# adaLN weights as one transfer per unit in two tiles, and the units placed at half chunks and partly in later sub-layers

## The chip, the cores and the metric

The kernel runs on one core of one Trainium2 chip. The time is the device time of one execution in microseconds (us). It was 2662.07 us before the change, the median of three runs that lie between 2660.03 and 2666.98 us. The profile is of one further execution, which took 2658.19 us. Engines are named as in the profile: PE (TensorE, with PEld for its weight loads), DVE (VectorE), ACT (ScalarE), POOL (GpSimd), SP (SyncE, which here only issues transfers).

## The reference

One inference step of two layers, for 512 prompt tokens and 8 sequences of 8 sample tokens that share all weights, so 576 tokens of width 1024 in float32. Each layer has three sub-layers: a SwiGLU FFN (`d_ff` 2816), a token mixer (layer 0 a Mamba-2 mixer, layer 1 sliding-window attention), and a second FFN. Every sub-layer is wrapped in norms that are modulated by the conditioning vector c of the sequence:

```python
cs = jax.nn.silu(c)
mod = (cs @ ada_w[i] + ada_b[i]).reshape(bsz, 1, N_SUB, 3, D_MODEL)      # shift, scale, gate of 3 sub-layers
hin = rms_norm(x, norm_pre[i, s]) * (1 + mod[:, :, s, 1]) + mod[:, :, s, 0]
f = swiglu(hin, ffn_w_in[i, si], ffn_w_out[i, si])                       # or the mixer, for s == 1
x = x + coef * mod[:, :, s, 2] * rms_norm(f, norm_post[i, s])            # coef 0.5 for an FFN, 1 for a mixer
```

The change concerns only `cs @ ada_w[i]`, the adaLN modulation: for each layer a matrix of 1024 x 9216 float32, 37.7 MB, which has to be read once and multiplied by nine vectors (one prompt, eight samples).

## The kernel before

**Stages.** The six sub-layers run one after another. They are named by layer and place: (0,0) is the first FFN of layer 0, (0,1) the Mamba mixer, (0,2) the second FFN, then (1,0), (1,1) (attention) and (1,2). An FFN goes through its 22 blocks of 128 hidden columns in four groups, `FFG`: 5, 5, 6 and 6 blocks. After each group `run_out` multiplies the group's hidden columns by their part of `w_out` and adds that to `f`. All large matrix products are three matmuls per 128x128 block, of a high and a low part of weights and activations (`whi`, `wlo`, made by ACT at line 441 or 607 and by DVE or POOL at line 444 or 603 from a raw tile that SP has loaded).

In the first group each weight block is used directly (`gemm_part` and `gemms`, lines 461 and 473). In the other three groups, 17 blocks, `seven` computes a block of the up and gate product from seven half-size products; here such a block is called a chunk. Its matmuls are those of line 628 (`prod`), 84 per chunk in seven products of 12, in this order: pa, pb, pc, pd, then pa, pc and pd again. The raw tiles `raw` and `rawu` of a chunk, 512 KB each, have two buffers each.

**The adaLN work.** The modulation of a layer is cut into five column groups q: q 0 to 3 have 2048 columns, q 4 has 1024 (only the gate of the third sub-layer). Each is cut into 8 units, one for each 128 rows of `ada_w` (`ada_unit`, line 150). A unit issues its transfers from ACT's queue (line 162), four of [128, 512] (256 KB; 128 KB for q 4) into tiles `adaw` of which there are `NADA` = 7, and after a `yield` does four matmuls (line 165), one for each quarter of the columns, which go to four different 32-row strips of one PSUM bank, `adaps`. The profile counts two PE records for one such matmul, so 8 for a unit. The eighth unit of a group then copies the bank to SBUF on ACT (`adasb`, line 169, which takes one of the seven `adaw` tiles), turns it with PE transposes (`adatp`, line 172) and adds the bias on DVE (`modraw`, line 178).

Group (0, 0) is made by another function at the start (`ada_first`). The others are spread over the FFNs by `during`: before the change 32 units in (0,0), 16 in (0,2) and 24 in (1,0). `Pend` hands them out. Its method `step` is called at certain places of an FFN (lines 510, 713, 714); at each call it adds `rate` = units / `nsteps` to a counter and starts one unit for each whole number in it. Starting a unit means: issue its transfers, then do the matmuls of the unit started before. An FFN has 38 such calls: 4 in the rest of the first group, and two together after each of the 17 chunks. `nsteps` is 40 for an FFN. `pend.flush` (line 717), after the last chunk, starts what is left. In (0,2) the adaLN units alternate with 16 units that copy the attention's bias table (`rel_unit`).

**The end of an FFN.** After the last chunk and the flush, the pool `ada` (with the `adaw` tiles and the scratch of `seven`) is closed, and `Boundary.open` loads the residual x. `run_out` then does the last `w_out` product, with four of its eight weight blocks in borrowed tiles `wx`, and beside it gathers the statistics of the norms on ACT, DVE and POOL (`stat`, lines 324 to 335), from which the next sub-layer's input `hin` is made (`sums`, `update`). Below, the *middle* of an FFN is the stretch from its first matmul of line 628 to the first matmul of its last `w_out` product, and its *tail* the stretch from there to the last matmul of that product.

**Order.** The kernel is written in a tile framework. A planner, with its own costs of instructions, sets the order in which each engine's instructions stand and which of the buffers of a tag each tile gets; an instruction may be moved ahead of its place in the program when its operands and a buffer are free by the planner's clock. At run time each engine takes its instructions in that order, and one that waits holds up what is behind it on its engine.

Of the kernel before, what the change touches and what calls it, by code (L numbers as in the profile page):

```python
# [20 lines left out]
EPS = 1e-6  # L21
NEG = -1e30
FFG = ((0, 5), (5, 5), (10, 6), (16, 6))
NADA = 7
NFINE = 24
PL = ((25, 48, 60), (25, 52, 64))
WR = 4
# [31 lines left out]
def body(ctx: ExitStack, tc: tile.TileContext, A, O):  # L59
# [90 lines left out]
    def ada_unit(l, q, k):  # L150
        n = 2048 if q < 4 else 1024
        if k == 0:
            if l and q == 0:
                mods[l] = keep.tile([128, 72, 9], F32, tag="modraw", name="modraw", bufs=2)
            mods[l, q] = ps_a.tile([128, 512], F32, tag="a", name="adaps")
        w = n // 4
        pt = mods[l, q]
        aw = []
        for j in range(4):
            c = q * 2048 + j * w  # L160
            aw.append(ap[0].tile([128, 512], F32, tag="adaw", name="adaw", bufs=NADA)[:, :w])
            nc.scalar.dma_start(aw[j], A["ada_w"][l, k * 128:(k + 1) * 128, c:c + w])
        yield
        for j in range(4):
            PE.matmul(out=pt[32 * j:32 * j + 32, :w], lhsT=cs[:, k, :], rhs=aw[j], start=(k == 0), stop=(k == 7))  # L165
        if k == 7:
            nt = w // 128
            sb = ap[0].tile([128, 512], F32, tag="adaw", name="adasb", bufs=NADA)
            S.copy(sb[:, :w], pt[:, :w])
            tp = ps_s.tile([128, 512], F32, tag="s", name="adatp")  # L170
            for t in range(nt):
                PE.transpose(tp[:, t * 128:(t + 1) * 128], sb[:, t * 128:(t + 1) * 128], ident)
            c0 = q * 16
            md = mods[l][:, c0:c0 + 4 * nt, :].rearrange("p (j t) s -> p t j s", t=nt)
            src = tp[:, :w].rearrange("p (t j s) -> p t j s", j=4, s=32)
            bia = adab[:, l, c0:c0 + 4 * nt].rearrange("p (j t) -> p t j", t=nt)
            for t in range(nt):
                V.tensor_tensor(out=md[:, t], in0=src[:, t, :, 0:9], in1=bia[:, t].unsqueeze(2).to_broadcast([128, 4, 9]),
                                op=ALU.add)
# [88 lines left out]

    def rel_table(pool):

        tab = pool.tile([128, 512], F32, tag="adaw", name="tab", bufs=NADA)[0:16, 0:HL]
        V.memset(tab, NEG)
        p = ps_s.tile([128, 512], F32, tag="s", name="tabp")
        PE.matmul(out=p[0:16, 0:129], lhsT=rb, rhs=oh, start=True, stop=True)
        V.tensor_copy(out=tab[:, 127:256], in_=p[0:16, 0:129])
        nc.scalar.dma_start(scr_t, tab)
# [312 lines left out]
        acts = lambda x: [(x[0][:, k], x[1][:, k]) for k in range(4)]  # L589
        return dict(b11=acts(b11), b21=acts(b21), b22=acts(b22), t1=acts(t1), t2=acts(t2), t3=acts(t3), t4=acts(b12))  # L590

    def seven(pool, mp, l, si, m, acts, mt):

        rg = wp.tile([128, 1024], F32, tag="raw", name="raw", bufs=2)
        ru = pool.tile([128, 1024], F32, tag="rawu", name="rawu", bufs=2)
        for i, r in enumerate((rg, ru)):
            nc.sync.dma_start(r, A["w_in"][l, si, m, :, i])
        a11, a12, a21, a22 = rg[:, 0:512], rg[:, 512:1024], ru[:, 0:512], ru[:, 512:1024]
        sc = pool.tile([128, 2048], F32, tag="scmb", name="scmb")
        s2, s1, s3, s4 = (sc[:, i * 512:i * 512 + 512] for i in range(4))  # L600

        def tt(e, out, a, b, op):
            e.tensor_tensor(out=out, in0=a, in1=b, op=op)  # L603

        def parts(w, c, src):
            n = src.shape[-1]
            S.copy(w[0][:, c:c + n], src)  # L607
            tt(V, w[1][:, c:c + n], src, w[0][:, c:c + n].bitcast(F32), ALU.subtract)

        ws = [[wp.tile([128, 1024], F32R, tag=t, name=t, bufs=WR) for t in ("whi", "wlo")] for _ in range(4)]  # L610
        parts(ws[0], 0, a11)
        tt(V, s1, a21, a22, ALU.add)
        tt(V, s3, a11, a21, ALU.subtract)
        tt(V, s2, s1, a11, ALU.subtract)
        parts(ws[0], 512, s2)
        parts(ws[1], 0, sc[:, 512:1536])
        tt(V, s4, a12, s2, ALU.subtract)
        parts(ws[2], 0, a12)
        parts(ws[2], 512, s4)
        parts(ws[3], 0, a22)  # L620
        pa, pb, pc, pd = (ps_g.tile([128, 512], F32, tag="g", name="g")[:, 0:N2] for _ in range(4))

        def prod(p, w, c, at, first):
            hi, lo = ws[w]
            for k in range(4):
                o = slice(c + k * 128, c + k * 128 + 128)
                for j, (wt, x) in enumerate(((lo, at[k][0]), (hi, at[k][1]), (hi, at[k][0]))):
                    mms.append(PE.matmul(out=p, lhsT=wt[:, o], rhs=x, start=(first and k == j == 0),  # L628
                                         stop=(k == 3 and j == 2), skip_group_check=True))

        def tile_(name):
            return pool.tile([128, N2], F32, tag="cmb", name=name, bufs=5)

        p1, u2, ur, ul = map(tile_, ("p1", "u2", "ur", "ul"))
        gl, gr = (mp.tile([128, 320], F32, tag="sil", name=n, bufs=3)[:, 0:N2] for n in ("gl", "gr"))

        def mid(t, g, u):
            hi, lo = (mt[:, j, t * N2:t * N2 + N2] for j in (0, 1))
            tt(V, u, g, u, ALU.mult)
            S.copy(hi, u)  # L640
            tt(V, lo, u, hi.bitcast(F32), ALU.subtract)

        prod(pa, 0, 0, acts["b11"], True)
        S.copy(p1, pa)
        prod(pb, 0, 512, acts["t2"], True)
        tt(V, u2, pb, p1, ALU.add)
        prod(pc, 1, 0, acts["t1"], True)
        tt(V, ur, pc, u2, ALU.add)
        prod(pd, 1, 512, acts["t3"], True)
        tt(V, ur, pd, ur, ALU.add)  # L650
        prod(pa, 2, 0, acts["b21"], False)
        S.activation(out=gl, in_=pa, func=AF.Silu)
        prod(pc, 2, 512, acts["b22"], False)
        tt(V, gr, pc, u2, ALU.add)
        S.activation(out=gr, in_=gr, func=AF.Silu)
        mid(1, gr, ur)
        prod(pd, 3, 0, acts["t4"], False)
        tt(V, ul, pd, u2, ALU.add)
        mid(0, gl, ul)


    def ffn(l, s, hin, f, pend, bd):
        si = 0 if s == 0 else 1
        sub = lambda name: tc.tile_pool(name=f"{name}{l}{s}", bufs=1, reuse_waits="tile")
        with sub("mid") as mp:
            hin_t = hins[-1]
            for gi, (m0, mk) in enumerate(FFG):
# [24 lines left out]
                if gi == 0:  # L692
                    for m in range(m0, m0 + mk):
                        items += mk_items(m)
                    with sub("fx") as fx:
                        run_in(hin, items[:FI], FI, borrow(fx, "wx", 2 * (FI - WR)), pend,
                               (lambda: first_half1(fx)) if (l, s) == (0, 0) else None,
                               pre if (l, s) == (0, 0) else ())
                    spill((l, s) != (0, 0))
                    ada_cm = sub("ada")  # L700
                    ap[0] = ada_cm.__enter__()
                    if (l, s) == (0, 0):
                        for t, a in later:
                            nc.sync.dma_start(t, a)
                    if (l, s) == (0, 2):
                        rel_table(ap[0])
                    run_in(hin, items[FI:], 0, None, pend)
                    acts = seven_acts(ap[0], hin_t)
                else:
                    for m in range(m0, m0 + mk):  # L710
                        mids.append(mp.tile([128, 2, T], F32R, tag="mid", name="mid", bufs=6))
                        seven(ap[0], mp, l, si, m, acts, mids[-1])
                        pend.step()
                        pend.step()
                if gi < len(FFG) - 1:
                    run_out(loads, halves(mids), f, gi == 0)
# [721 lines left out]

    def x_sums(h):
        t0, n = HALF[h]  # L1440
        xacc = tmp.tile([128, 320], F32, tag="dg", name="xacc", bufs=2)
        for k in range(8):
            sq_add(xacc[:, 0:256], x[h][:, k, :], 256, k == 0)
            if h == 1:
                sq_add(xacc[:, 256:n], x[2][:, k, :], 64, k == 0)
        nb = len(offsets(n))
        ps = ps_s.tile([128, 512], F32, tag="s", name="ssq")
        token_sums(ps, 0, xacc[:, :n], n)
        V.tensor_scalar(out=sx[h], in0=ps[:, :nb], scalar1=1.0 / 1024, scalar2=None, op0=ALU.mult)
        v = small("v0")[:, :nb]  # L1450
        G.tensor_tensor(out=v, in0=sx[h], in1=epsc[:, :nb], op=ALU.add)
        return rsqrt(v, nb)
# [17 lines left out]
    def first_half1(pool):  # L1470
# [1 line left out]
        norm_sample(pool, mv, r_half1, hin)  # L1472


    during = {(0, 0): [(0, 1), (0, 2), (0, 3), (0, 4)], (0, 1): [], (0, 2): [(1, 0), (1, 1)],
              (1, 0): [(1, 2), (1, 3), (1, 4)], (1, 1): [], (1, 2): []}
    nsteps = {0: 40, 1: 20, 2: 40}
    for l in range(2):
        for s in range(3):
            us = [u for lq in during[l, s] for u in units(*lq)]  # L1480
# [162 lines left out]
```

## Time and profile before

| | |
|---|---|
| median of three runs | 2662.07 us |
| the profiled execution | 2658.19 us, of which the span from the first to the last instruction is 2656.4 us |
| PE busy | 2500.6 us (94%), mean granted clock 0.966 |
| DVE, ACT, POOL busy | 1820.5 us (69%), 1149.3 us (43%), 344.5 us (13%) |
| HBM read, written | 301.70 MB, 29.67 MB; 125 GB/s over the span |
| transfers into `adaw` | 224 of 256 KB, 64 of 128 KB, all on ACT's queue |

Busy times are sums over the span. A row of the timeline or of the chain of waits begins with its start in us from the span's start and its length; a row of grouped instructions begins with line, engine and operation. "x8" is a count of instructions. A row of busy time by window has the stretch and its length, then the busy us and the instructions of PE, PEld, DVE, ACT and POOL, PE's granted clock as a share of 2.4 GHz, the mean busy share of the 16 DMA engines and GB/s. What stands in square brackets behind a row is the time that the engine was idle before it, and what ended that.

### The profile page before, as it was taken

How to read it: one execution, taken by the hardware profiler on the slowest of the kernel's cores; microseconds unless marked ns; L12 is line 12 of the kernel's file. 1: busy time of each engine (PE TensorE's matmuls, PEld its weight loads, DVE VectorE, ACT ScalarE, POOL GpSimd, SP SyncE). 2: the span in 40 equal slices, each digit the busy share in tenths (PEclk: the TensorE clock that was granted, in tenths of full speed). 3: DMA queues.
4: the chain of work that ended last, by engine and by line, in shares of the span. 5: the costliest groups of instructions: out<-in, count | busy, mean ns of one | idle time of the engine just before them, and what ended most of it. 6: DMA issues, size and time to landing. Idle time of an engine off the chain costs nothing.

```text
span 2656.4 us, 45760 instructions
## 1 busy us (share of the span) xinstructions
PE 2500.6 (94%) x18037; PEld 2301.2 (87%) x18037; DVE 1820.5 (69%) x3361; ACT 1149.3 (43%) x2400; POOL 344.5 (13%) x476
## 2 busy tenths in 40 slices
PE   7999999789999999799999989999988998999997
PEld 5989788677888887799999889899978868999997
DVE  5566656598758677866677585766747677677685
ACT  3343324445545453534343443433443565343343
POOL 2000000432313122600000230000013006000001
PEclk8999999999999999899999989999998998999998
DMA  6444544333443434163343423535334312222323
GB/s 240 147 141 151 173 131 137 110 116 96 138 128 95 137 112 156 62 194 125 123 159 112 137 103 118 171 131 166 104 120 156 109 41 95 96 87 89 96 76 107
DMA packets 150606, 331.13 MB, mean 125 GB/s; under 512 B 21231, under 2 KB 51551, under 8 KB 146943
## 3 DMA queue, kind: packets, MB, share of 16 engines
q1 hardware_dynamic: 100535, 245.52, 28.9%
q10 hardware_dynamic: 49856, 82.69, 9.5%
q8 instruction: 141, 2.31, 0.4%
q14 instruction: 74, 0.61, 0.1%
HBM read 301.70 MB, written 29.67 MB: 125 GB/s over the span
## 4 chain that ended last, share of the span: by engine, by line
PE 77%; DVE 7%; DMA 7%; issue 3%; ACT 3%; POOL 2%; SPq 0%; ACTq 0%; DVEq 0%; POOLq 0%
PE g L473 41%; PE g L628 27%; DMA adaw<-in_ada_w 3%; PE adaps L165 2%; DMA w<-scr_a 1%; DVE st L335 1%; DMA adaf<-in_ada_w 1%; DVE acc L818 1%; POOL wlo L444 1%; POOL stt L331 1%; DVE hin L411 1%; PE po L1255 1%; PE py L902 1%; PE rb L255 1%; DMA raw<-in_w_out 1%
## 5 line engine op out<-in xcount | busy, mean ns | idle before, releaser
L473 PE MATMUL g<-hin,whi 128*128 128x320 f32 (+1 forms) x2880 | 608.9, 307 | 14.3 <-DVE hin L411 14.3
L473 PEld LDWEIGHTS g<-hin,whi 128*128 128x128 f32 x2880 | 481.6, 197 | 24.7 <-DVE hin L411 17.7
L473 PE MATMUL g<-mid,whi 128*128 128x320 f32 (+1 forms) x2432 | 491.8, 297 | 0.0
L473 PE MATMUL g<-hin,wlo 128*128 128x320 f32 (+1 forms) x1440 | 442.3, 312 | 27.5 <-ACT hin L410 10.6
L628 PE MATMUL g<-hin,whi 128*128 128x288 f32 x2176 | 436.3, 294 | 0.0
L473 PEld LDWEIGHTS g<-mid,whi 128*128 128x128 f32 x2432 | 391.8, 189 | 7.7 <-issue 7.0
L473 PE MATMUL g<-mid,wlo 128*128 128x256 f32 (+1 forms) x1216 | 361.0, 298 | 0.1
L628 PEld LDWEIGHTS g<-hin,whi 128*128 128x128 f32 x2176 | 348.9, 188 | 0.0
L628 PE MATMUL g<-tcmb,whi 128*128 128x288 f32 x1632 | 331.6, 297 | 0.0
L628 PE MATMUL g<-hin,wlo 128*128 128x288 f32 x1088 | 325.0, 299 | 0.0
L473 PEld LDWEIGHTS g<-hin,wlo 128*128 128x128 f32 x1440 | 281.0, 197 | 48.4 <-issue 15.5
L441 ACT CAST whi<-raw 128x1024 fp32r<-128x1024 f32 (+2 forms) x220 | 199.2, 906 | 252.4 <-PE g L473 144.5
L444 DVE TENSOR_TENSOR wlo<-raw,whi 128x1024 fp32r<-128x1024 f32 (+3 forms) x200 | 206.2, 1033 | 117.8 <-ACT whi L441 117.0
L628 PEld LDWEIGHTS g<-tcmb,whi 128*128 128x128 f32 x1632 | 265.9, 191 | 8.9 <-issue 8.9
L628 PE MATMUL g<-tcmb,wlo 128*128 128x288 f32 x816 | 243.3, 298 | 0.0
L473 PEld LDWEIGHTS g<-mid,wlo 128*128 128x128 f32 x1216 | 228.7, 188 | 11.3 <-issue 8.7
L628 PEld LDWEIGHTS g<-hin,wlo 128*128 128x128 f32 x1088 | 204.1, 188 | 30.1 <-issue 24.3
L525 DVE TENSOR_TENSOR f<-g,f 128x256 f32<-128x256 f32 (+1 forms) x240 | 108.8, 455 | 159.9 <-PE g L473 158.9
L607 ACT CAST whi<-scmb 128x512 fp32r<-128x512 f32 (+1 forms) x204 | 153.9, 761 | 142.6 <-PE g L628 83.8
L603 DVE TENSOR_TENSOR wlo<-scmb,whi 128x512 fp32r<-128x512 f32 (+1 forms) x204 | 175.1, 865 | 39.7 <-ACT whi L607 39.6
L331 POOL TENSOR_TENSOR st<-x,f 128x256 f32<-128x256 f32 x10 | 10.0, 998 | 1362.1 <-ACT f L325 809.3
L607 ACT CAST whi<-raw 128x512 fp32r<-128x512 f32 x136 | 84.5, 622 | 203.7 <-PE g L628 125.7
(294 smaller groups left out, 4025.4 us busy)
## 6 DMA issues: line engine op xcount, KB each, us to landing
adaw<-in_ada_w ACTq DMA_DIRECT2D x224, 256.0 KB, 5.7
raw<-in_w_in SPq DMA_DIRECT2D x108, 512.0 KB, 3.6
rawu<-in_w_in SPq DMA_DIRECT2D x68, 512.0 KB, 5.3
raw<-in_w_out SPq DMA_DIRECT2D x64, 384.0 KB, 3.1
raw<-in_w_out SPq DMA_DIRECT2D x64, 320.0 KB, 2.9
raw<-in_w_ssm SPq DMA_DIRECT2D x40, 512.0 KB, 3.7
x_dram<-x SPq DMA_DIRECT2D x10, 1024.0 KB, 3.9
x<-x_dram SPq DMA_DIRECT2D x10, 1024.0 KB, 6.7
```

The costliest lines, as they stand in the source:

```text
L165: PE.matmul(out=pt[32 * j:32 * j + 32, :w], lhsT=cs[:, k, :], rhs=aw[j], start=(k == 0), stop=(k == 7))
L255: ins = PE.matmul(out=r[:, c:e], lhsT=mul(y[:, i:i + 1], [128, 128]), rhs=ident[:, 128 - (e - c):128], start=True, stop=True)
L331: G.tensor_tensor(out=st[:, 2, :256], in0=x_cur[h][:, o, :], in1=fs[:, 0:256], op=ALU.mult)
L335: V.tensor_tensor(out=self.acc[h][:, :ns], in0=self.acc[h][:, :ns], in1=st[:, :ns, :n], op=ALU.add)
L411: V.scalar_tensor_tensor(out=hin[h][:, 1, k, :256], in0=tm, scalar=mv["sh"][:, k, 0:1], in1=hin[h][:, 0, k, :256].bitcast(F32), op0=ALU.ad ...
L441: S.copy(hi[:, :n], raw[:, :n])
L444: i = (V if early and c < PSP else eng or V).tensor_tensor(out=lo[:, c:e], in0=raw[:, c:e], in1=hi[:, c:e].bitcast(F32), op=ALU.subtract)
L473: mms.append(PE.matmul(out=p[:, :n], lhsT=wt[:, a:b], rhs=at, start=(k == j == 0), stop=(j == 2 and k == K - 1)))
L525: V.tensor_tensor(out=fs, in0=p, in1=fs, op=ALU.add)
L603: e.tensor_tensor(out=out, in0=a, in1=b, op=op)
L607: S.copy(w[0][:, c:c + n], src)
L628: mms.append(PE.matmul(out=p, lhsT=wt[:, o], rhs=x, start=(first and k == j == 0), stop=(k == 3 and j == 2), skip_group_check=True))
```

## The change

A unit fetches its 128 rows in one transfer of [128, 2048] (1024 KB; 512 KB for q 4) into one of two tiles; the four matmuls read quarters of it. `adasb` gets a tag with one buffer of its own, which `rel_table` uses too. One of the two calls of `step` per chunk moves from the chunk's end to behind its third product (pc), after 36 of the 84 matmuls. `during` now has 24 units in (0,0), 16 in (0,2), 24 in (1,0) and 8 in (1,2): q 4 of either layer is moved to the third sub-layer, the only one that uses it, and one group of layer 1 from (0,2) to (1,0). `nsteps` of an FFN is 34 in place of 40. The tile `xacc` of the start moves from the pool `tmp` to the first `ada` pool.

```diff
-NADA = 7
@@ ada_unit
-        aw = []
-        for j in range(4):
-            c = q * 2048 + j * w
-            aw.append(ap[0].tile([128, 512], F32, tag="adaw", name="adaw", bufs=NADA)[:, :w])
-            nc.scalar.dma_start(aw[j], A["ada_w"][l, k * 128:(k + 1) * 128, c:c + w])
+        aw = ap[0].tile([128, 2048], F32, tag="adaw", name="adaw", bufs=2)[:, :n]
+        nc.scalar.dma_start(aw, A["ada_w"][l, k * 128:(k + 1) * 128, q * 2048:q * 2048 + n])
         yield
         for j in range(4):
-            PE.matmul(out=pt[32 * j:32 * j + 32, :w], lhsT=cs[:, k, :], rhs=aw[j], start=(k == 0), stop=(k == 7))
+            PE.matmul(out=pt[32 * j:32 * j + 32, :w], lhsT=cs[:, k, :], rhs=aw[:, j * w:j * w + w], start=(k == 0),
+                      stop=(k == 7))
...
-            sb = ap[0].tile([128, 512], F32, tag="adaw", name="adasb", bufs=NADA)
+            sb = ap[0].tile([128, 512], F32, tag="adasb", name="adasb", bufs=1)
@@ rel_table
-        tab = pool.tile([128, 512], F32, tag="adaw", name="tab", bufs=NADA)[0:16, 0:HL]
+        tab = pool.tile([128, 512], F32, tag="adasb", name="tab", bufs=1)[0:16, 0:HL]
@@ seven
         prod(pc, 1, 0, acts["t1"], True)
         tt(V, ur, pc, u2, ALU.add)
+        pend.step()
         prod(pd, 1, 512, acts["t3"], True)
@@ ffn
-                        seven(ap[0], mp, l, si, m, acts, mids[-1])
-                        pend.step()
+                        seven(ap[0], mp, l, si, m, acts, mids[-1], pend)
                         pend.step()
@@ x_sums
-        xacc = tmp.tile([128, 320], F32, tag="dg", name="xacc", bufs=2)
+        xacc = ap[0].tile([128, 320], F32, tag="xacc", name="xacc", bufs=2)
@@ body
-    during = {(0, 0): [(0, 1), (0, 2), (0, 3), (0, 4)], (0, 1): [], (0, 2): [(1, 0), (1, 1)],
-              (1, 0): [(1, 2), (1, 3), (1, 4)], (1, 1): [], (1, 2): []}
-    nsteps = {0: 40, 1: 20, 2: 40}
+    during = {(0, 0): [(0, 1), (0, 2), (0, 3)], (0, 1): [], (0, 2): [(0, 4), (1, 0)],
+              (1, 0): [(1, 1), (1, 2), (1, 3)], (1, 1): [], (1, 2): [(1, 4)]}
+    nsteps = {0: 34, 1: 20, 2: 34}
```

## Rows read from the trace of the kernel before

**Rows 1.** The page's chain of work that ended last, by line.

```profile
PE g L473 41%; PE g L628 27%; DMA adaw<-in_ada_w 3%; PE adaps L165 2%; DMA w<-scr_a 1%; DVE st L335 1%; DMA adaf<-in_ada_w 1%; DVE acc L818 1%; POOL wlo L444 1%; POOL stt L331 1%; DVE hin L411 1%; PE po L1255 1%; PE py L902 1%; PE rb L255 1%; DMA raw<-in_w_out 1%
```

**Rows 2.** Busy time by window: middle, tail of (0,0), (0,2), (1,0), (1,2); stretch, length.

```profile
140.27:459.00 318.73, 304.11 (x2185) 271.71 (x2183) 201.06 (x376) 114.26 (x204) 0.00 (x0) 0.98 0.45 147
459.00:522.78 63.78, 52.73 (x341) 44.98 (x339) 27.88 (x46) 25.35 (x55) 23.32 (x30) 0.95 0.39 130
1212.74:1490.25 277.51, 277.51 (x2081) 262.68 (x2079) 199.23 (x366) 113.24 (x203) 0.00 (x0) 1.00 0.41 133
1490.25:1536.90 46.65, 44.28 (x317) 42.78 (x314) 26.35 (x44) 24.45 (x51) 21.35 (x28) 0.96 0.38 134
1657.85:1947.89 290.04, 286.44 (x2140) 265.28 (x2138) 199.15 (x370) 113.72 (x203) 0.00 (x0) 1.00 0.43 140
1947.89:2007.65 59.76, 49.72 (x325) 44.79 (x323) 28.42 (x47) 25.38 (x55) 23.12 (x30) 0.91 0.36 121
2338.22:2598.41 260.19, 260.15 (x1958) 259.47 (x1957) 195.86 (x358) 112.70 (x200) 0.00 (x0) 1.00 0.29 89
2598.41:2642.70 44.29, 41.40 (x298) 40.65 (x296) 24.63 (x52) 18.98 (x38) 3.29 (x3) 0.96 0.32 114
```

**Rows 3.** The same windows, PE's `adaps` matmuls alone: length, busy (records), clock, DMA.

```profile
140.27:459.00 318.73, 35.67 (x214) 0.98 0.45 147
459.00:522.78 63.78, 7.50 (x29) 0.95 0.39 130
1212.74:1490.25 277.51, 15.70 (x118) 1.00 0.41 133
1490.25:1536.90 46.65, 1.11 (x5) 0.96 0.38 134
1657.85:1947.89 290.04, 23.27 (x174) 1.00 0.43 140
```

**Rows 4.** Who waited for the tile `adaw`, whole span: us in total, times.

```profile
  PEld adaps L165: 30.6, 24
  PE adaps L165: 24.1, 23
```

**Rows 5.** PE's timeline at a chunk end of (0,0) with two units.

```profile
163.80 1.92 PE L165 MATMUL adaps<-adaw,cs 128*32 128x512 f32 x14
...
170.41 1.91 PE L165 MATMUL adaps<-adaw,cs 128*32 128x512 f32 x2 [2.64 <-DMA adaw<-in_ada_w]
```

**Rows 6.** ACT's timeline at the same place.

```profile
174.63 0.62 ACT L607 CAST whi<-raw 128x512 fp32r<-128x512 f32 x1 [6.13 <-DMA adaw<-in_ada_w]
```

**Rows 7.** PE's timeline: two neighbouring chunk ends of (0,2), and a half-width unit.

```profile
1223.95 1.06 PE L165 MATMUL adaps<-adaw,cs 128*32 128x512 f32 x8
...
1236.27 1.06 PE L165 MATMUL adaps<-adaw,cs 128*32 128x512 f32 x8
...
1897.83 0.64 PE L165 MATMUL adaps<-adaw,cs 128*32 128x256 f32 x8
```

**Rows 8.** ACT's timeline in the tails of (0,0) and (0,2).

```profile
477.56 0.37 ACT L169 COPY adasb<-adaps 128x256 f32<-128x256 f32 x1 [16.05 <-PE adaps L165]
...
1495.07 0.84 ACT L441 CAST wx<-raw 128x768 fp32r<-128x768 f32 x1 [0.80 <-PE adatp L172]
```

**Rows 9.** The page's transfers of 1 MB: size, median us to landing.

```profile
x_dram<-x SPq DMA_DIRECT2D x10, 1024.0 KB, 3.9
x<-x_dram SPq DMA_DIRECT2D x10, 1024.0 KB, 6.7
```

**Rows 10.** Landing of `rawu`: in chunks of (0,2), then in chunks of (1,2).

```profile
DMA to landing us min/median/max: 3.8/5.4/6.7
...
DMA to landing us min/median/max: 3.6/3.7/4.7
```

**Rows 11.** A `raw` load's issue in SP's timeline, and its first cast in ACT's.

```profile
1223.89 0.33 SPq L597 DMA_DIRECT2D raw<-in_w_in  x1
...
1240.79 0.62 ACT L607 CAST whi<-raw 128x512 fp32r<-128x512 f32 x1 [1.16 <-PE g L628]
```

More of the change, by code (lines that the diff above doesn't have):

```diff
@@ L590, in seven_acts, with seven @@
         return dict(b11=acts(b11), b21=acts(b21), b22=acts(b22), t1=acts(t1), t2=acts(t2), t3=acts(t3), t4=acts(b12))
-    def seven(pool, mp, l, si, m, acts, mt):
+    def seven(pool, mp, l, si, m, acts, mt, pend):
         rg = wp.tile([128, 1024], F32, tag="raw", name="raw", bufs=2)
```

## The prediction

> **What bounds the kernel now.** I read the chain of waits first [rows 1]: 68% of the span is PE in the matmuls of lines 473 and 628, and the adaLN work has two entries, 3% for the landing of `adaw` and 2% for its matmuls. The chain charges a transfer from its issue on, also while PE still works, so 3% (80 us) is too much. The waits on the tile show why to be careful [rows 4]: 24.1 us in 23 stops of PE; the 30.6 us of its weight loads are the same stops seen a second time. But a stop costs more than its idle time, and ACT is held too. So the price of the adaLN work is best read by stage.
>
> For that the busy times by window [rows 2] give a clean ruler: (1,2) has the same FFN without one unit, and its middle takes 260.19 us with PE busy in 260.15. The other middles take 58.5 us more in (0,0), 17.3 in (0,2) and 29.8 in (1,0). Divide by the units in them, eight records each [rows 3]: 214/8 = 26.75 units, 14.75 and 21.75. That is 2.19, 1.17 and 1.37 us for a unit. In (0,2), with one unit per chunk, PE is busy in all of the 277.51 us, so 1.17 us is a unit without any stall (1.06 us of matmuls [rows 7], a bubble, and its share of the transposes). In (0,0) a unit costs nearly twice that.
>
> PE's timeline there shows how [rows 5]: two units fall together at a chunk's end. Seven matmuls (x14) run at once, the eighth waits 2.64 us, and then takes 1.91 us alone, when four together take 1.06 [rows 7]. Two units need eight tiles and there are seven: the eighth transfer can be issued only when the first tile is free, just before it is needed. ACT issues the transfers in order and is held with them: its next cast comes after 6.13 us idle [rows 6]. The granted clock of that middle is 0.98 against 1.00 [rows 2].
>
> The second place is the tail. It takes 63.78 us in (0,0) and 59.76 in (1,0), against 46.65 in (0,2) [rows 2]. Of the 38 calls of `step`, rates of 0.8 and 0.6 leave two units to the flush and one to be finished. In (0,0) ACT stands 16.05 us idle in front of the copy `adasb` [rows 8], and behind that copy on ACT are the casts of the `wx` weights and the statistics. The copy starts 18.6 us into the tail (477.56 − 459.00); in (0,2) the first `wx` cast, which follows such a copy, starts 4.8 us into it (1495.07 − 1490.25).
>
> **The change part by part.**
>
> *One transfer, two whole tiles.* A tile is now free as soon as its unit's matmuls are over, so the transfer for the unit after next is issued then. That the planner moves an issue up to where its buffer comes free is in the trace: seven tiles were ready at 163.80 [rows 5]. So a unit's transfer has at least two half chunks, one chunk of 12.3 us (1236.27 − 1223.95) [rows 7]. No row has a load of 1 MB in rows of 8 KB into this tile. Nearest are 1 MB transfers of x: 3.9 us written, 6.7 read behind others [rows 9]. Up to 12 us the cost is nothing and no end makes it negative; I take the read, 6.7, and cost 0. What hides it is the 84 matmuls of a chunk; without them it would be 6.7 us per unit. The stalls of (0,0) and (1,0) then go, and what is late next is nothing on PE: DVE, the next busiest engine, has 201 of 319 us. Three issues of four go from ACT's queue as well; ACT is busy 114 of 319 us and off the path, so 0.
>
> *Half chunks.* A unit behind pc costs PE the same four matmuls. After it pd comes, whose bank is its own; DVE's add of pc runs beside it. Extra cost between 0 and 0.11 us per unit (the difference of 1.17 and 1.06, if all of it came twice); (0,2) has its stops between products too, so I take 0. A wait there would hold the casts for the next chunk behind the issue on ACT, but the raw tiles give the casts 16.9 us from issue to use [rows 11].
>
> *Rates and places.* 24, 32, 24 and 8 units over 34 steps are all started by the 34th or 35th of 38 calls and finished one later. None is left to the flush. In the first group's four calls (0,0) now finishes one unit, not two: −1.1 us; (0,2) a half one: −0.4. A unit of q 4 costs 1.17 − (1.06 − 0.64) = 0.75 us [rows 7]. The middles over 260.2 become:
> (0,0): 23 × 1.17 = 27.0 in place of 58.5, −31.5;
> (0,2): 7 × 0.75 + 8 × 1.17 = 14.6 in place of 17.3, −2.7;
> (1,0): 27.0 in place of 29.8, −2.8;
> (1,2): 8 × 0.75, +6.0.
>
> *Tails.* Without units the first cast of `wx` and the statistics no longer stand behind an adaLN copy. (0,2) still has 1.11 us of unit matmuls in its tail [rows 3], so 45.5 us is what such a tail takes clean; (1,2), whose end differs, has 44.29 [rows 2]. That gives −18.3 in (0,0), −14.3 in (1,0), −1.1 in (0,2). Ends: nothing (another wait holds the tail) and −37 (all as (1,2)). I take the first sum, −33.7, since (0,2) runs the same code.
>
> *`adasb`, `tab`, `xacc`.* One buffer more or another pool; each copy waits for the transposes of a group eight units back. 0 from both sides: nothing else uses those buffers at that time.
>
> The sum is −31.5 − 1.1 − 2.7 − 0.4 − 2.8 + 6.0 − 33.7 = −66.2 us. The profiled execution (2658.19, of which 2656.4 span) becomes 2592. It lies 3.9 us below the median of the runs, so against that median I say 2596.
>
> A rule of the Trainium skill speaks against one large transfer: its page "DMA: Bandwidth & Descriptors", section "Queues, rings and completion order", says that an engine takes turns between queue rows packet by packet. By it rows of 8 KB from ACT's queue could take two bytes for each of SP's 4 KB rows while both are in flight, and `rawu` would land, as an estimate, after 3 × 3.7 = 11 us. The trace has today's share: 5.4 us beside 1 MB of `adaw` per chunk, 3.7 without [rows 10]. Both are below the 16.9 us of lead [rows 11], so the sum stands by either.
>
> **The rivals.**
>
> 1. *The lead is half of what I count* (the issue stays at its place in the program, one step ahead). For it: a buffer of 1 MB may be placed by the planner differently from small ones. Against it stands the place of the issues [rows 5]. Then the lead is 36 or 48 of 84 matmuls of 11.15 us, plus the unit: 5.8 or 7.4 us, against 6.7. Of 23 gaps in an FFN 13 are one step long, about six of them the short kind: 0.9 us each in two FFNs, 11 us: 2607. Each further us of landing adds 26: 2630 at the most.
>
> 2. *The tails keep half.* Another wait, the load of x or of `wx`, is nearly as late as the copy was. For it: PE idles in (1,2)'s tail too, 44.29 against 41.40 busy. Against: (0,2). Half of 32.6 is 16: 2612.
>
> 3. *Slower: the weight loads starve.* The 1 MB block in flight delays `raw` and `rawu` of the same chunk past their use. It decides from 16.9 us of landing on. At 19 us each of the 51 chunks with units would wait 2 us: +102 − 66 gives 2698. For it: landing grew from 3.7 to 5.4 with units. Against: the DMA engines are busy 0.41 to 0.45 of the middles [rows 2], and in (0,2) that growth cost PE nothing.
>
> 4. *It does not do what it says*: the planner moves the unit at the half chunk back beside the other. Then two whole tiles are ready at once and nothing stalls: 2600; or the waits return elsewhere: about 2662.
>
> **How the numbers follow.** The forecast has 0.75, rival 1 0.07, rival 2 0.10, rival 3 0.05, rival 4 0.03 (a third of it no change). The forecast's own range is 2584 (all tails as in (1,2), and the runs' own 3 us) to 2606. Rivals 1 and 2 put the upper end at 2626; below 2584 and above 2626 about 0.15 is left. About 0.3% is what a measurement can tell from no change. Faster has 0.92, the same 0.03 (rival 4, or a weak form of rival 3), slower 0.05.
>
> **What would show it.** Right: all `adaps` matmuls in clusters of eight records without idle time before them; middles of about 287, 275, 287 and 266 us; no `adasb` copy in a tail, the first `wx` cast some 5 us into each, and tails near 45.5. Waits on `adaw` under 3 us in all. Rival 1 shows in waits of about 1 us before clusters at half chunks; rival 2 in tails above 52 with another releaser; rival 3 in idle time of ACT's casts behind `raw`. I would be wrong first of all in the tails, where I take one stage's value for two others.

## The result and the profile after

The changed kernel takes 2596.84 us, the median of four runs from 2593.56 to 2598.61, against 2661.45 before (four runs now, 2660.03 to 2666.98): a ratio of 0.9765, interval 0.9748 to 0.9783. The forecast was 2596 us. Its profiled execution took 2598.61 us, of which 2596.8 are span. From one profiled execution to the other that is 59.6 us less, where the sum said 66.2. That the median is met so closely is partly luck, the scatter of single executions: before's profiled one lay 3.3 us below its median, after's lies 1.8 above.

First the page after: the chain by line, then the two kinds of transfers at issue with KB and median us to landing. The entry for the landing of `adaw`, 3% in [rows 1], is gone; a unit's 1 MB lands in 6.7 us, and `rawu` in 4.5.

```profile
PE g L470 41%; PE g L625 29%; PE adaps L161 2%; DVE st L332 1%; DMA adaf<-in_ada_w 1%; DMA w<-scr_a 1%; DVE acc L815 1%; POOL wlo L441 1%; POOL stt L328 1%; DVE wlo L441 1%; DVE hin L408 1%; PE po L1252 1%; PE py L899 1%; ACT whi L438 1%; PE rb L252 1%
...
adaw<-in_ada_w ACTq DMA_DIRECT2D x56, 1024.0 KB, 6.7
...
rawu<-in_w_in SPq DMA_DIRECT2D x68, 512.0 KB, 4.5
```

The same eight windows as [rows 2], in the same order (middle and tail of (0,0), (0,2), (1,0), (1,2)). In the middles PE's busy time is now all of the stretch but for 0.66 us in (0,0), and the clock is 1.00 in each. In the tails of (0,0), (0,2) and (1,0) PE is idle for 4.8 to 5.7 us of 49 and has a clock of 0.93 to 0.97.

```profile
140.16:429.05 288.89, 288.23 (x2155) 265.29 (x2154) 199.45 (x374) 113.16 (x203) 0.00 (x0) 1.00 0.46 156
429.05:478.20 49.15, 44.37 (x312) 43.61 (x311) 29.02 (x46) 26.17 (x54) 21.63 (x30) 0.93 0.37 134
1163.35:1438.76 275.41, 275.40 (x2085) 263.00 (x2083) 198.12 (x366) 112.86 (x202) 0.00 (x0) 1.00 0.37 124
1438.76:1487.76 49.00, 43.31 (x312) 42.29 (x311) 28.93 (x46) 26.13 (x54) 21.66 (x30) 0.97 0.38 134
1605.34:1893.26 287.92, 287.92 (x2155) 265.28 (x2153) 199.46 (x374) 112.98 (x203) 0.00 (x0) 1.00 0.46 157
1893.26:1941.71 48.45, 43.35 (x312) 42.35 (x311) 28.89 (x46) 26.05 (x54) 21.58 (x30) 0.96 0.39 136
2273.11:2539.05 265.94, 265.93 (x2024) 261.27 (x2023) 196.69 (x361) 113.09 (x201) 0.00 (x0) 1.00 0.30 98
2539.05:2583.26 44.21, 41.53 (x298) 40.85 (x296) 24.50 (x52) 18.88 (x38) 3.29 (x3) 0.96 0.30 114
```

The `adaps` matmuls alone in the four middles (stretch, length, busy us and records, clock, DMA share, GB/s), which answer to [rows 3]: 23, 15, 23 and 8 units, and none in a tail.

```profile
140.16:429.05 288.89, 24.30 (x184) 1.00 0.46 156
1163.35:1438.76 275.41, 12.99 (x120) 1.00 0.37 124
1605.34:1893.26 287.92, 24.30 (x184) 1.00 0.46 157
2273.11:2539.05 265.94, 4.91 (x64) 1.00 0.30 98
```

Who waited for `adaw` after, over the span (us, times), and its landing: PE's 24.1 us [rows 4] are gone, and of the 30.6 of its weight loads 0.8 are left. ACT's wait is that of the copy `adasb` for the last matmuls of its group.

```profile
  ACT adasb L166: 10.6, 7
  PEld adaps L161: 0.8, 2
...
DMA to landing us min/median/max: 3.2/6.3/9.4
```

PE's timeline after, at the place of [rows 5]: two units of one chunk, 6 us apart, each in one cluster of 1.06 us without idle time before it. At 404.40 two units still fall together, and even there nothing waits, since both have a tile.

```profile
164.89 1.07 PE L161 MATMUL adaps<-adaw,cs 128*32 128x512 f32 x8
...
170.84 1.06 PE L161 MATMUL adaps<-adaw,cs 128*32 128x512 f32 x8
...
404.40 1.92 PE L161 MATMUL adaps<-adaw,cs 128*32 128x512 f32 x16
```

Where the 59.6 us went, window by window (span to span):

| | predicted | measured |
|---|---|---|
| middles (0,0), (0,2), (1,0), (1,2) | −31.5, −2.7, −2.8, +6.0 | −29.8, −2.1, −2.1, +5.75 |
| tails (0,0), (0,2), (1,0), (1,2) | −18.3, −1.1, −14.3, 0 | −14.6, +2.35, −11.3, −0.1 |
| everything else | −1.5 | −7.6 |

So the middles gave 28.3 us of the 31.0 foreseen, the tails 23.7 of 33.7. "Everything else" is mainly −4.8 from the end of (0,0)'s tail to (0,2)'s middle and −3.4 from the end of (0,2)'s tail to (1,0)'s middle.

### The profile page after: what moved, and what is told of

Same layout as the page of the kernel before. It is cut to its first block, busy times and chain, and to the rows that moved or that the text cites. A ratio compares the mean times of both kernels' runs of the same rounds, so it can differ in the third digit from the quotient of the medians.

```text
span 2596.8 us, 45412 instructions
## 1 busy us (share of the span) xinstructions
PE 2472.2 (95%) x18037; PEld 2292.6 (88%) x18037; DVE 1818.5 (70%) x3361; ACT 1149.6 (44%) x2400; POOL 339.8 (13%) x476
## 4 chain that ended last, share of the span: by engine, by line
PE 79%; DVE 8%; DMA 4%; issue 3%; ACT 3%; POOL 3%; SPq 0%; POOLq 0%; DVEq 0%; ACTq 0%
PE g L470 41%; PE g L625 29%; PE adaps L161 2%; DVE st L332 1%; DMA adaf<-in_ada_w 1%; DMA w<-scr_a 1%; DVE acc L815 1%; POOL wlo L441 1%; POOL stt L328 1%; DVE wlo L441 1%; DVE hin L408 1%; PE po L1252 1%; PE py L899 1%; ACT whi L438 1%; PE rb L252 1%
## 5 line engine op out<-in xcount | busy, mean ns | idle before, releaser
L625 PEld LDWEIGHTS g<-tcmb,wlo 128*128 128x128 f32 x816 | 153.3, 188 | 23.0 <-DVE ur L600 18.4
```

## The experiments

Three questions were open: which part of the change does the work, whether the tails were shortened for the reason given (no unit in the flush), and what holds the tails at 49 us in place of 45.5. All times are medians beside runs of the kernel before on the same chip; the ratio and its interval are against those. "Tails" and "middles" stand in the order (0,0), (0,2), (1,0), (1,2).

### The old places in the new tiles, and the new places in the old tiles

```diff
  (changed kernel)
-    during = {(0, 0): [(0, 1), (0, 2), (0, 3)], (0, 1): [], (0, 2): [(0, 4), (1, 0)],
-              (1, 0): [(1, 1), (1, 2), (1, 3)], (1, 1): [], (1, 2): [(1, 4)]}
-    nsteps = {0: 34, 1: 20, 2: 34}
+    during = {(0, 0): [(0, 1), (0, 2), (0, 3), (0, 4)], (0, 1): [], (0, 2): [(1, 0), (1, 1)],
+              (1, 0): [(1, 2), (1, 3), (1, 4)], (1, 1): [], (1, 2): []}
+    nsteps = {0: 40, 1: 20, 2: 40}
```

> The changed kernel with the units in their old sub-layers and at the old rate (40 steps), all else as changed. My theory: a large part of the gain was the flush that is gone, so the tails of (0,0) and (1,0) grow again, from 49 us to 55 to 64 each, by waits of ACT's adasb copy in the tail; the middles keep their 1.2 us per unit. Time 2612 to 2628. Rival (the tail was long because of the seven tiles, not because of units left over): tails stay within 3 us of 49, time 2595 to 2602.

Measured: 2594.99 us (2594.44 to 2601.22), ratio 0.9737 (0.9696 to 0.9778). My expectation of the time missed; it came out at the lower end of the rival's range. Three windows of this kernel's profile, (0,0)'s tail and (1,2)'s middle and tail, and below them ACT's timeline in (0,0)'s tail:

```profile
435.10:491.98 56.88, 47.29 (x332) 45.63 (x329) 28.50 (x46) 25.15 (x55) 22.12 (x30) 0.91 0.39 135
...
2278.95:2539.16 260.21, 260.20 (x1958) 259.54 (x1957) 195.70 (x358) 112.54 (x200) 0.00 (x0) 1.00 0.28 88
2539.16:2579.07 39.91, 39.85 (x298) 39.30 (x296) 24.25 (x52) 19.01 (x38) 3.30 (x3) 1.00 0.20 67
```

```profile
445.30 0.37 ACT L166 COPY adasb<-adaps 128x256 f32<-128x256 f32 x1 [7.89 <-PE adaps L161]
```

The mechanism that I named is there: the copy `adasb` is back in the tail, 10.2 us into it, and that tail is 7.7 us longer than after's. (1,0)'s, at 50.43, is only 2.0 longer, as the rival said. Against the kernel before, the two tails are 6.9 and 9.3 us shorter with the old places, so a large part of what they gained in the change comes from its other parts. And without units (1,2) is 5.7 us shorter in its middle and 4.3 in its tail, and (0,2)'s tail takes 45.12. The middles and tails add up to 0.9 us less than after's. The new places shift time from these two tails to other windows.

The counterpart, before's kernel with the new `during` and `nsteps` alone:

> The kernel before with only the new sub-layers of the units and 34 steps; seven small tiles and both steps at the chunk's end stay. My theory: the tails lose 24 us as in the changed kernel, (0,0) has 24 full units with about seven pairs in its middle (300 to 305 us), and (1,0) gets the same, 300 to 305 in place of 290; time 2625 to 2642. Rival (places are worth little without the tiles): within 8 us of the kernel before.

Measured: 2650.65 us (2640.24 to 2660.5), ratio 0.9956 (0.9932 to 0.998): slower than I expected, and both large middles are longer than the 300 to 305 us that I gave them. The windows of the two large middles and their tails, and then who waited for `adaw` on PE in the same kernel:

```profile
139.66:448.94 309.28, 299.71 (x2154) 268.11 (x2153) 199.79 (x374) 113.54 (x203) 0.00 (x0) 0.99 0.45 147
448.94:497.04 48.10, 43.20 (x312) 42.45 (x311) 29.04 (x46) 26.24 (x54) 21.63 (x30) 0.96 0.40 137
...
1619.11:1932.01 312.90, 301.92 (x2155) 270.17 (x2153) 199.81 (x374) 113.51 (x203) 0.00 (x0) 0.98 0.44 145
1932.01:1980.70 48.69, 43.36 (x312) 42.34 (x311) 28.93 (x46) 26.04 (x54) 21.57 (x30) 0.96 0.39 136
```

```profile
  PE adaps L165: 20.1, 14
```

The tails fall to 48 to 49 us, as in the changed kernel: with no unit left to the flush they shorten in these tiles too. The middle of (1,0) grows by 22.9 us, since its units now come in pairs and stop PE as those of (0,0) did. As a part alone the places are worth 12.8 us by the medians (more than the rival's 8); on top of the other parts, nothing that the first run of this pair shows.

### Which part of the tiles

Before's kernel with `NADA = 8` and the new buffers for `adasb`, `tab` and `xacc`; the places, the four transfers of a unit and `nsteps` stay.

```diff
-NADA = 7
+NADA = 8
-            sb = ap[0].tile([128, 512], F32, tag="adaw", name="adasb", bufs=NADA)
+            sb = ap[0].tile([128, 512], F32, tag="adasb", name="adasb", bufs=1)
...
```

> The kernel before with eight small tiles in place of seven and a buffer of its own for adasb and the table (and xacc in the first pool); transfers of 256 KB, places and rates of before. My theory: the eighth tile takes the wait out of the pairs, so the middle of (0,0) falls from 319 to 288 to 296 us and that of (1,0) to 285 to 289; the tails keep the flush but lose part of the wait, 50 to 62; time 2612 to 2632. Rival (the single large transfer is what counts): the middle of (0,0) stays above 310, time above 2645.

Measured: 2600.57 us (2599.01 to 2604.28), ratio 0.9755 (0.9714 to 0.9795): faster than either range. Middle and tail of (0,0) and (1,0):

```profile
140.01:427.80 287.79, 287.79 (x2187) 266.52 (x2185) 200.44 (x376) 114.01 (x204) 0.00 (x0) 1.00 0.49 162
427.80:488.15 60.35, 50.80 (x340) 44.43 (x337) 28.07 (x47) 24.89 (x55) 23.01 (x30) 0.94 0.40 135
...
1616.51:1899.14 282.63, 282.52 (x2142) 264.69 (x2140) 198.59 (x369) 112.97 (x203) 0.00 (x0) 1.00 0.44 143
1899.14:1955.82 56.68, 47.35 (x324) 43.47 (x321) 28.98 (x48) 25.62 (x55) 23.01 (x30) 0.94 0.36 126
```

The stops in the middles are gone, with four small transfers and all units at chunk ends. The tails of (0,0) and (1,0) keep their 60 and 57 us, and yet nearly the whole gain is there. The next two take this apart: the eighth tile with `adasb` still among the tiles, and then seven tiles with `adasb` on its own. `xacc` is moved in both.

> The kernel before with eight small tiles in place of seven, adasb still taking one of them (and xacc in the first pool, for the space). My theory: the eighth tile alone takes the wait out of the pairs, but for the one unit in eight where adasb holds a tile: middle of (0,0) 288 to 296 us, time 2600 to 2612. Rival (the buffer of its own for adasb did it): middle of (0,0) above 312, time above 2640.

Measured: 2602.36 us (2598.34 to 2607.84), ratio 0.9783 (0.9754 to 0.9812); middles 287.84, 277.46, 282.46 and 260.21.

> The kernel before with seven small tiles and a buffer of its own for adasb and the table, xacc in the first pool. My theory: pairs still lack the eighth tile, so the middle of (0,0) stays at 310 to 320 us and the time at 2640 to 2665. Rival (adasb's buffer did it): 2600 to 2612.

Measured: 2649.86 us (2648.25 to 2655.05), ratio 0.9958 (0.9942 to 0.9975); middles 319.58 and 289.68 in (0,0) and (1,0), as before, with 16.77 and 3.19 us of stops. Of the 59 us that the first of these two gains, 47.5 are missing in the second (2649.86 − 2602.36), which has the same space but keeps the eighth tile for `adasb`. `adasb`'s buffer on top of the eighth tile shows nothing (ratios of 0.9755 and 0.9783, with overlapping intervals). The 12 us that the second keeps can come from `xacc` or, with seven tiles, from `adasb`'s buffer; `xacc` was then moved alone.

```diff
  (kernel before)
-        xacc = tmp.tile([128, 320], F32, tag="dg", name="xacc", bufs=2)
+        xacc = ap[0].tile([128, 320], F32, tag="xacc", name="xacc", bufs=2)
```

> The kernel before with only xacc moved to the first pool. My theory: the 2.5 KB that this frees in every later stage let x be loaded early in (1,2), whose tail falls from 44.3 to 40 us, and nothing else changes: 3 to 8 us faster than the kernel before. Rival (a larger part of the gain of e3 and e6 sits here): 9 to 15 us faster.

Measured: 2652.08 us (2645.73 to 2662.08), ratio 0.9977 (0.9963 to 0.9991). SP's loads of x in layer 1 (duration min/median/max, first and last start) in this kernel, then in the kernel before:

```profile
L94 SPq DMA_DIRECT2D x<-x_dram x6: 326/423/431, 2175.2 to 2265.7; - x6
```

```profile
L94 SPq DMA_DIRECT2D x<-x_dram x6: 326/402/434, 2183.5 to 2603.2; - x6
```

The last load of x in the kernel before is issued at 2603.2, 4.8 us into (1,2)'s tail. Here it is issued at 2265.7, before (1,2)'s middle begins at 2330.33. The 2560 bytes per partition that `xacc` gave back to `tmp` leave room for x early, and the tail falls from 44.29 to 39.82 us. By the medians this kernel gains 6.3 us of the 12, within the range expected; what the other half is stays open. `adasb`'s buffer with seven tiles was not run alone, and the intervals of the two ratios overlap, so it may be nothing.

This kernel differs from the one with eight tiles and a shared `adasb` by `NADA` alone: they gain 6.3 and 59.2 us, each beside its own runs of the kernel before, so one tile more is worth 53 us. With `adasb` on its own in both it is 51 (62.9 against 11.8). In the changed kernel the early load of x is lost again: (1,2) has the two `adaw` tiles, and its tail takes 44.21.

### One tile, and four transfers into two

```diff
  (changed kernel)
-        aw = ap[0].tile([128, 2048], F32, tag="adaw", name="adaw", bufs=2)[:, :n]
+        aw = ap[0].tile([128, 2048], F32, tag="adaw", name="adaw", bufs=1)[:, :n]
```

> The changed kernel with one tile of 1 MB in place of two, so a transfer can be issued only when the unit before it is over and has one step, not two. My theory (the second tile is what hides the landing of 6.7 us): in (0,0) and (1,0) the units one step after another wait about 1 us at the short half chunk and next to nothing at the long one, and a late matmul costs its clock besides; waits on adaw 10 to 30 us in all, time 2606 to 2630. Rival (a half chunk is enough to hide it): within 4 us of the changed kernel.

Measured: 2646.78 us (2638.6 to 2648.94), ratio 0.9943 (0.992 to 0.9967): the direction was right, the size larger than expected. Its windows of (0,0) and (1,0), then one of the stops on PE with the windows behind it, then the waits:

```profile
140.48:445.01 304.53, 291.85 (x2155) 267.40 (x2153) 197.75 (x374) 112.65 (x203) 0.00 (x0) 0.99 0.45 151
...
1626.34:1928.75 302.41, 291.71 (x2154) 267.19 (x2153) 197.68 (x374) 112.88 (x203) 0.00 (x0) 0.99 0.45 153
```

```profile
175.56 1.94 PE L161 MATMUL adaps<-adaw,cs 128*32 128x512 f32 x8 [3.94 <-DMA adaw<-in_ada_w]
```

```profile
175.50:177.50 2.00, 1.95 (x9) 0.28 (x9) 0.00 (x0) 0.00 (x0) 0.00 (x0) 0.50 0.00 0
177.50:179.00 1.50, 1.50 (x7) 1.50 (x8) 0.00 (x0) 0.00 (x0) 0.00 (x0) 0.55 0.55 87
179.00:181.00 2.00, 2.00 (x17) 2.00 (x17) 0.46 (x1) 0.00 (x0) 0.00 (x0) 1.00 0.83 332
```

```profile
  PE adaps L161: 24.6, 14
```

The reader sees why a stop costs more than its wait: behind 3.94 us of idle time the cluster takes 1.94 us in place of 1.07, and the granted clock is 0.50 there, 1.2 of 2.4 GHz, and 1.00 again in the window from 179.00. Over the whole middle it is 0.99. Of the 30.1 us that the two middles lose, 22.7 are more idle time (12.68 + 10.70 − 0.66) and 7.4 are slower work (PE busy 291.85 and 291.71 in place of 288.23 and 287.92). The tails of (0,0), (0,2) and (1,0) add 1.7, 2.6 and 2.9 us. SP issues the load of x later in each of them, by 1.1, 1.3 and 1.5 us, which would fit what is found on the tails below; that it is the cause is not shown, since (1,2)'s tail, with x 0.5 us later, is 1.0 us shorter.

The other way round, the changed kernel with a unit's megabyte fetched in four transfers into the same two tiles:

```diff
-        nc.scalar.dma_start(aw, A["ada_w"][l, k * 128:(k + 1) * 128, q * 2048:q * 2048 + n])
+        for j in range(4):
+            nc.scalar.dma_start(aw[:, j * w:j * w + w], A["ada_w"][l, k * 128:(k + 1) * 128, q * 2048 + j * w:q * 2048 + j * w + w])
```

> The changed kernel with the unit's 1 MB fetched by four transfers of 256 KB into the same two tiles. My theory (the space of two whole units is what counts, not the size of a transfer): no wait on adaw in the middles, time within 5 us of the changed kernel. Rival (fewer, larger transfers are worth something by themselves, by ACT's queue or by their landing): slower by more than 8 us.

Measured: 2599.55 us (2595.47 to 2608.14), ratio 0.9779 (0.9762 to 0.9797). Beside it ran the changed kernel again:

> The changed kernel itself once more, as the measure for the three beside it on this chip: 2592 to 2601 us.

Measured: 2601.47 us (2593.65 to 2602.42), ratio 0.9784 (0.9764 to 0.9803), half a us above the range. One transfer or four makes no difference that these runs show; the room for two whole units is what counts. The Trainium skill ("DMA: Bandwidth & Descriptors", section "Bandwidth", under "Measured") advises batching transfers to at least 1 MiB to get at least 75% of peak bandwidth, from transfers that GpSimd issued. No run here shows the bandwidth of the two kinds alone, but where the landing is hidden the larger one bought no time.

### Both steps at the chunk's end

```diff
  (changed kernel)
         tt(V, ur, pc, u2, ALU.add)
-        pend.step()
         prod(pd, 1, 512, acts["t3"], True)
...
                         seven(ap[0], mp, l, si, m, acts, mids[-1], pend)
                         pend.step()
+                        pend.step()
```

> The changed kernel with both steps of a chunk at the chunk's end again. My theory: with two whole tiles a pair of units finds both tiles loaded, so no PE time is lost: waits on adaw under 5 us in all, middle of (0,0) within 4 us of 289, time within 6 us of the changed kernel. Rival (the half-chunk place is what hides the transfers): pairs wait 1 to 3 us each in (0,0) and (1,0), about seven pairs in either, time 2607 to 2630.

Measured: 2596.4 us (2595.78 to 2599.04), ratio 0.9739 (0.9699 to 0.9779); middles 288.01, 275.09, 288.48 and 265.75; PE waits 2.8 us for `adaw`. The half-chunk place does spread the units as the change says, but with room for two units the pair at the chunk's end is as good.

### What holds the tails

All units of layer 0 (and q 0 of layer 1) in (0,0), the rest of layer 1 in (1,0), none in (0,2) and (1,2), in the new tiles. The bias table `tab`, which took the `adasb` buffer, goes to a scratch tile.

```diff
  (changed kernel)
...
-    during = {(0, 0): [(0, 1), (0, 2), (0, 3)], (0, 1): [], (0, 2): [(0, 4), (1, 0)],
-              (1, 0): [(1, 1), (1, 2), (1, 3)], (1, 1): [], (1, 2): [(1, 4)]}
-    nsteps = {0: 34, 1: 20, 2: 34}
+    during = {(0, 0): [(0, 1), (0, 2), (0, 3), (0, 4), (1, 0)], (0, 1): [], (0, 2): [],
+              (1, 0): [(1, 1), (1, 2), (1, 3), (1, 4)], (1, 1): [], (1, 2): []}
+    nsteps = {0: 36, 1: 20, 2: 34}
...
```

> The changed kernel with no units in (0,2) and (1,2): 40 units in (0,0) at 36 steps, 32 in (1,0), and the bias table built in another scratch tile, so that the pool of (0,2) and (1,2) has no adaLN tile. My theory from e1 and e4, where the x load of (1,2) found free room, was issued before the last w_out loads and the tail took 39.9 us, not 44.2: the tails of (0,2) and (1,2) fall by 4 to 5 us each and the middles only trade units, time 2584 to 2592. Rival (the pairs in (0,0), now 1.1 units per step, lose it again in waits): 2594 to 2604.

Measured: 2590.24 us (2582.7 to 2595.09), ratio 0.9733 (0.9702 to 0.9764); tails 48.96, 43.37, 48.97 and 39.96. Where the FFN has no `adaw` tiles its tail falls by 4 to 6 us; with them it stays at 49. The last experiment gives the tiles back early: they and `adasb` lie in a pool of their own, which is flushed and closed a chunk before the end.

```diff
  (the kernel just above)
...
+                    aw_cm = sub("adw") if pend.u else None
+                    apw[0] = aw_cm.__enter__() if aw_cm else None
...
                         pend.step()
+                        if aw_cm and m == 20:
+                            pend.flush()
+                            aw_cm.__exit__(None, None, None)
...
-    nsteps = {0: 36, 1: 20, 2: 34}
+    nsteps = {0: 34, 1: 20, 2: 34}
```

> e8 and, in (0,0) and (1,0), the adaLN tiles in a pool of their own that is closed one chunk before the last, so that the x load finds room there too. My theory (a clean tail is set by the x load, issued 2.6 us into it and landing in 6 to 9 us): the tails of (0,0) and (1,0) fall from 49 to 43 to 45, time 4 to 10 us below e8, 2578 to 2588. Rival (the tail is set by the casts and sums of its own, the x load only happens to be last): tails within 1.5 us of 49, time within 3 us of e8.

Measured: 2580.13 us (2578.25 to 2586.58), ratio 0.9714 (0.9695 to 0.9733). First the changed kernel's profile in (0,0)'s tail, which begins at 429.05: SP's timeline, then the chain of waits, then POOL's timeline and PE's.

```profile
417.95 13.89 SPq L436 DMA_DIRECT2D raw<-in_w_out  x5
431.89 2.15 SPq L93 DMA_DIRECT2D x<-in_xT  x3
435.56 1.71 SPq L436 DMA_DIRECT2D raw<-in_w_out  x2
```

```profile
431.89 5.65 DMA x<-in_xT
```

```profile
437.88 0.74 POOL L328 TENSOR_TENSOR st<-x,f 128x256 f32<-128x256 f32 x1 [389.72 <-ACT stt L321]
...
446.46 7.24 PE L470 MATMUL g<-mid,wx 128*128 128x256 f32 x36 [3.62 <-DVE wx L441]
```

Then this last kernel: SP's timeline around the start of the tail at 451.24, and the windows of middle and tail of (0,0) and (1,0).

```profile
424.79 0.33 SPq L437 DMA_DIRECT2D raw<-in_w_out  x1
432.66 2.25 SPq L93 DMA_DIRECT2D x<-in_xT  x3
440.14 13.55 SPq L437 DMA_DIRECT2D raw<-in_w_out  x5
```

```profile
144.78:451.24 306.46, 302.53 (x2272) 269.55 (x2271) 199.51 (x380) 112.77 (x205) 0.00 (x0) 0.99 0.54 189
451.24:494.63 43.39, 41.68 (x312) 40.90 (x311) 28.36 (x46) 26.01 (x54) 23.62 (x30) 1.00 0.30 97
...
1598.87:1892.05 293.18, 293.18 (x2213) 266.98 (x2212) 200.97 (x376) 113.86 (x204) 0.00 (x0) 1.00 0.51 173
1892.05:1936.41 44.36, 41.92 (x312) 40.91 (x311) 28.15 (x46) 25.95 (x54) 23.55 (x30) 1.00 0.30 96
```

In the changed kernel SP issues the load of x 2.8 us into the tail, behind five `w_out` loads that it issues over 13.89 us; x lands at 437.54, and the statistics on POOL begin at 437.88. DVE sums them up before it makes the low part of the next `wx` at 445.45, and for that PE stands idle for 3.62 us. In the last kernel x is issued 18.6 us ahead of the tail, and all four tails take 39.8 to 44.4 us at a clock of 1.00. The edit moves the flush and the pool's end together, but of SP's loads around (0,0)'s tail only x moved: the five `w_out` loads begin 11.1 us ahead of the tail in both kernels, the other two 6.5 and 6.2 us into it. So a late load of x holds the tails, and x finds no room while the `adaw` tiles are open. It is also the version that beats both: 21 us faster than the changed kernel beside it, 78 faster than the kernel before. Some 7 us of that are this last edit by the two kernels' gains (78.2 against 71.4 for the one before it), 10 us by the windows of the two tails; the rest came with the places.

## Why the prediction came out as it did

**The stops: right, by the mechanism named.** Two units need eight tiles and there were seven. The waits on PE fell from 24.1 us to nothing, and one tile of 256 KB more, with all else as it was, is worth 51 to 53 us. The clusters of eight without idle time, and middles of 288.9, 275.4, 287.9 and 265.9 against about 287, 275, 287 and 266, came as said.

**A unit of 1.17 us: a little small for the half chunks.** 23 units take 28.7 us over 260.2 in (0,0), 1.25 each, and 27.7 in (1,0), 1.20. I costed the half-chunk place at nothing. With pairs at the chunk's end and eight small tiles 27 units take 27.6 us, 1.02 each (287.79 − 260.15): the pair of clusters takes 1.92 us where two single ones take 2.12. With both steps at the chunk's end but large tiles it is 1.14 net of the stops ((288.01 − 260.2 − 1.65)/23). The difference, 2 to 5 us per large FFN, stayed below what the time of the whole shows.

**The transfer: right at cost 0.** The 1 MB transfer lands in 6.7 us as the median (6.3 with the half-sized ones), 9.4 at the most, well under the 12.3 us of a chunk; the 6.7 taken from the load of x was met. Rivals 1 and 3 are out by that: no wait of 1 us before the clusters, and no `raw` tile late enough to hold PE, which is busy in all but 0.66 us of the middles. By the rule of the Trainium skill that was weighed there ("DMA: Bandwidth & Descriptors", section "Queues, rings and completion order") the estimate for `rawu` was 11 us. The trace does not bear that estimate out: the median went from 5.9 to 5.7 us in (0,0)'s middle and from 5.4 to 4.3 in (0,2)'s, with 8.8 at the most.

**The tails: the mis-sized term.** The step that failed is "so 45.5 us is what such a tail takes clean", from (0,2) of the kernel before. Clean of units the tails of FFNs with `adaw` tiles take 48.0 to 49.3 us, in five kernels of these runs alike (the changed one twice, the new places alone, both steps at the chunk's end, and the one with all units in (0,0) and (1,0)); 48.9 to 50.7 with four transfers, and 50.9 to 51.6 with one tile. Two things misled me. PE's timeline of the kernel before, just ahead of that tail's start at 1490.25, has

```profile
1488.40 1.92 PE L165 MATMUL adaps<-adaw,cs 128*32 128x512 f32 x14
```

Nearly two units of PE's work stand between the last chunk and the tail, while ACT, DVE and SP had already gone on: the load of x is issued 0.65 us into that tail, 2.64 into after's. The 46.65 us had a head start of some 2 us, and counted from the last chunk the stretch is about as long as after's 49.00 (46.65 + 1.92 = 48.57). Two kernels do not fit this wholly: with the old places in the new tiles, or in eight small ones and `adasb` on its own, the same count gives 47 us (45.12 and 45.04, and 1.92 each). With `adasb` among the eight it gives 48.1. Why two of them take less stays open. And the wait next in line was not the first `wx` cast, which starts 3.7 us into after's first tail, but the load of x, rival 2's mechanism. It keeps 10 us of the 33.7 foreseen rather than half; its threshold was 52 us, and the tails stayed below.

**The places: right in each window, but not a gain.** Each of the terms was there: no unit in the flush, −11 to −15 us in two tails (of which −7 in (0,0) and −9 in (1,0) came with the old places as well), +5.75 in (1,2). What the sum did not have is what the places take away. With the old ones in the new tiles (1,2) has no `adaw` tiles, x is loaded early, and its tail takes 39.91 us; (0,2)'s takes 45.12, with the head start. I had taken (1,2)'s 44.29 as fixed. Since that benefit needs room which the kernel before did not have (`xacc` had it), no row of before showed the 39.91; but x's load at 2603.2, inside (1,2)'s tail, could have been read there.

**What made up for it.** The tails gave 10 us too little, the middles 2.7, and the rest of the program 6.1 too much. In the stretch from (0,0)'s tail to (0,2)'s middle, the mixer and the first group of (0,2), where little of the change works, the kernels of these runs take between 681 and 690 us with no order that I can see; before's 689.96 is the highest. Of the 4.8 us there 0.4 was said, for half a unit less ahead of (0,2)'s middle; the rest is no result of a step that I predicted, and its cause stays open. The −1.1 for one unit less ahead of (0,0)'s middle did not show: 8 records of its matmuls stand there in place of 16, and yet the middle begins at 140.16 in place of 140.27. The 3.4 us behind (0,2)'s tail belong with that tail: together they went from 167.60 to 166.58 us, −1.0, where −1.1 was said. So the errors partly cancel: from span to span the sum was 6.6 us too high.

## What to carry to other kernels

Count the buffers against the largest burst that one point of the program issues: seven tiles for two units of four cost some 50 us, one more tile gave them back, and neither larger transfers nor places at half chunks added to it. When a wait is taken away from a stretch, look for what is issued last in it before taking another stretch as its clean length, and look whether that other stretch started with work already done. And see which buffers are open at the moment at which the next stage's load wants its room: closing two tiles one chunk earlier took about 5 us off each of two tails.

## What the runs showed of the hardware that was not expected

A stopped PE loses twice: behind a stop of 2.64 us [rows 5] one matmul took 1.91 us, and behind one of 3.94 us a cluster of eight records took 1.94 in place of 1.07, at a granted clock of 0.50. The same shows in the tails: with 4.8 to 5.7 us of stops their granted clock is 0.93 to 0.97 and PE's busy time 43.3 to 44.4 us, without them 1.00 and 41.7 to 41.9, for the same 312 instructions. So in (0,0)'s tail 2.7 of the 5.8 us that the early load of x gave are PE's own busy time at the lower clock.

Room in SBUF acted at a distance in time: 2560 bytes per partition freed in the kernel before moved a load of x from 2603.2 to 2265.7 us and shortened a tail by 4.5 us.
